# A fifth tile for the rows fetched by the first chunk's expert retrieval, in slots 16 to 59

## The chip, the core and the metric

The kernel runs on one core of one Trainium2 chip. The metric is the device time of one execution in microseconds (us); the median of 3 runs of the kernel before is 1491.55 us (1486.63 to 1492.42). Five engines work side by side, each through its own list of instructions in a fixed order: PE multiplies matrices into PSUM, DVE (VectorE) works element by element, ACT (ScalarE) evaluates functions, POOL (GpSimd) issues the indirect fetches and some small operations, and SP issues most of the plain transfers. Between the engines there are only semaphores; a transfer is split over 16 DMA engines that all queues share.

## The reference

One layer is computed for 512 prompt tokens and 32 sample tokens (8 sequences of 4), model width 1024, all in float32. The first half is a token mixer: one projection `w_in` gives q, k, v, a gate and two convolution inputs; four retention heads and a causal convolution of width 31 with a layer norm run beside each other; `w_out` brings both together, and a residual with layer norm gives x1. The second half is a product-key expert retrieval (PEER) on x1, followed by a residual and a layer norm:

```
q  = x1 @ w_query                           # 8 heads, 2 x 128 each
v1, i1 = top16(q1 @ sub_keys_1); v2, i2 = top16(q2 @ sub_keys_2)
sv, ci = top16(v1[:, None] + v2[None, :])   # 16 of 16 x 16 sums
idx  = i1[ci // 16] * 128 + i2[ci % 16]     # one of 16384 experts
act  = gelu(peer_u[idx] . x1)
ffn  = sum(softmax(sv) * act * peer_v[idx]) # over 8 x 16 = 128 slots a token
```

So each token uses 128 experts, one in each of 128 slots, and an expert is a row of `peer_u` and a row of `peer_v`, 4 KB each.

## The kernel before

**Two ways to do the retrieval.** The tokens are cut into four groups. For the first prompt chunk (128 tokens), the 32 sample tokens and the second prompt chunk (128 tokens) the kernel fetches rows: for slot k, one indirect DMA of POOL brings for each partition (a token) the row of u and v of its expert, 8 KB, into a tile `g` of 128 x 2048 (1 MB); DVE makes the dot product with x1 (L652), ACT the GELU (L663) and the gate (L664), and DVE adds the weighted v row to an accumulator `acc` (L669). That is 128 slots for the first chunk, 32 for the samples (four slots beside each other on 128 partitions) and 128 for the second chunk. For the last 256 prompt tokens the kernel computes all 16384 experts densely: scores against each block of 128 experts (`scores_of`, L913), weights scattered from the lists by one-hot products (`build`, L1040, with DVE making `A`, `M`, `B` and multiplying the result into the G tiles at L1069), and the product with v (`v_products`, L1097).

**Stages.** The front computes the mixer: the first chunk and the samples first, then the lists of the first chunk (`retrieve`, in pairs of heads), then the mixer of the remaining 416 columns. Its end is `mix_b`, four layer norms with transposes (L532) that give `x1T`. Then come the query projections and key scores for all later tokens, the top-16 lists, the dense scores of experts 52 to 95 (`early_keys`), then `first_keys` (experts 0 to 51, with the scattered weights for experts 0 to 95), and `phases`, the products with v and the last 32 blocks.

**The first chunk's slots.** `gather(x1_0, ...)` (L634) is a generator; the first KX = 48 slots are traced at the end of the front, the other 80 after the dense early part, ahead of `first_keys`. The order on each engine is made by a planner at build time that goes by order of tracing as priority and by its own estimate of durations, so that slots fill holes in the work of the front. A slot can be fetched as soon as its tile is free. The pool `gp` has three tiles, each fourth slot below KX takes the one tile of pool `gx`; from slot 48 on only `gp` is used. A fetch of slot k thus waits for the accumulation of slot k-4, later of k-3.

**hold.** `hold(k, ins)` (L630) puts all dot products of the first chunk from slot k on behind instruction `ins` on DVE: `conv_norm`'s last multiplication (slot 47), the head norms of chunks 2 and 3 (slots 48 and 52), and the four layer norms of `mix_b` (54, 56, 59, 60). It is an order on one engine without a semaphore.

**Memory.** Pools on the left side stand in the order `per`, `gp`, `gw`, then those of the front (`gx`, `fe`, `wk`), which are closed after the first KX slots are traced; on their place come `uvp` (the ring for blocks of u and v), the G tiles and the lists' scratch. On the right side lie `wp` (four weight tiles) and, before, `sel`: the scratch of the first chunk's lists and one tile `keys` of 8 KB for each partition, which later serves as room for states and for two of the layer norms. In `gather` the choice of tile is one line:

```
pool = gx if k < KX and k % 4 == 3 else gp
```

Of the kernel before, what the change touches and what calls it, by code (L numbers as in the profile page):

```python
# [8 lines left out]
F32 = mybir.dt.float32  # L9
# [11 lines left out]
D = 1024  # L21
# [11 lines left out]
ND = NR - NG2  # L33
TB = 8
GS = 2.0 ** 13
KX = 48
UV = 4
FREE = 30
TB_AT = (30, 34, 56, 80)
# [59 lines left out]
def tile_step(ctx: ExitStack, tc: tile.TileContext, a, o):  # L99
# [4 lines left out]
    gp = ctx.enter_context(tc.tile_pool(name="gp", bufs=3))  # L104
    gw = ctx.enter_context(tc.tile_pool(name="gw", bufs=3))
    wps, right = ExitStack(), ExitStack()
    wp = wps.enter_context(tc.tile_pool(name="wp", bufs=4, side="right", reuse_waits="tile"))
    sel = [right.enter_context(tc.tile_pool(name="sel", bufs=2, side="right"))]
    dr = ctx.enter_context(tc.tile_pool(name="dr", bufs=1, space=bass.MemoryType.DRAM))
    front = ExitStack()  # L110
    gx = front.enter_context(tc.tile_pool(name="gx", bufs=1, reuse_waits="tile"))
# [7 lines left out]
    def mmps():  # L119
        turn[0] += 1  # L120
        return banks[turn[0] % len(banks)].tile([128, 512], F32, name="mm")
# [50 lines left out]
    def behind(ins, other):  # L172
        tc.add_manual_dep(ins.ins, other.ins.name, mybir.DependencyInfo(
            mybir.DependencyClass.NoSync, mybir.DependencyReason.DATA), reason="order")
# [5 lines left out]
    def small(name, shape, dt=F32, bufs=2):  # L180
        return wk.tile(shape, dt, name=name, bufs=bufs)
# [117 lines left out]
    def conv_s(y, after):  # L299

        yp = y.rearrange("p m (b i) -> p m b i", b=SB)
        for k in range(CK):
            w = dw[:, :, k].unsqueeze(2).unsqueeze(3).to_broadcast([128, 4, SB, SQ])
            if k == 0:
                behind(G.tensor_tensor(yp, u_s[:, :, :, 0:SQ], w, op=OP.mult), after)
                G.tensor_tensor(y, y, dwb.unsqueeze(2).to_broadcast([128, 4, NS]), op=OP.add)
                continue
            t = small("tap_s", [128, 4, SB, SQ], bufs=1)
            G.tensor_tensor(t, u_s[:, :, :, k:k + SQ], w, op=OP.mult)
            G.tensor_add(yp, yp, t)  # L310

    def conv_norm(y, n):

        pm = mmps()
        for m in range(4):
            T.matmul(pm[:, :n], onesm, y[:, m, :n], start=(m == 0), stop=(m == 3))
        pv = mmps()
        for m in range(4):
            V.tensor_sub(y[:, m, :n], y[:, m, :n], pm[:, :n])
            sq = small("sg", [128, 416], bufs=1)  # L320
            S.activation(sq[:, :n], y[:, m, :n], AF.Square)
            T.matmul(pv[:, :n], onesm, sq[:, :n], start=(m == 0), stop=(m == 3))
        rs = small("ropeB", [128, 416], bufs=1)
        S.activation(rs[:, :n], pv[:, :n], AF.Sqrt, bias=eps_c)
        V.reciprocal(rs[:, :n], rs[:, :n])
        for m in range(4):
            last = V.tensor_mul(y[:, m, :n], y[:, m, :n], rs[:, :n])
            S.activation(y[:, m, :n], y[:, m, :n], AF.Silu, bias=cg_b[:, m:m + 1], scale=cg_g[:, m:m + 1])
        return last

    bv, steps = [None], {}
# [33 lines left out]
    def gate_heads(on, n, gT, c0):  # L365
        pt = mmps().rearrange("p (h t) -> p h t", h=H)
        for h in range(H):
            T.transpose(pt[:, h, :n], on[:n, h * DH:(h + 1) * DH], ident[:n, :n])
        V.tensor_mul(gT[:, :, c0:c0 + n], gT[:, :, c0:c0 + n], pt[:, :, :n])
# [164 lines left out]
        return last  # L534

    def keys_or_scratch():
        return sel[0].tile([128, 2 * D], F32, name="keys", bufs=1)

    keys = []

# [87 lines left out]
    def hold(k, ins):  # L628

        held[k] = ins  # L630

    def gather(x1, idx, gate, acc, slots):

        late = len(slots) == 128 and x1 is not x1_0  # L634
        for k in slots:
            if x1 is x1_0:
                pool = gx if k < KX and k % 4 == 3 else gp
            elif late:
                pool = (gp, gp, gp, gx2[0])[k % 4] if k < 60 else (gp, gp, gp, gx2[0], bx)[k % 5]
            else:  # L640
                pool = gp if k < FREE else (gp, gp, gp, gx2[0])[k % 4]
            t = pool.tile([128, 2 * D], F32, name="g")
            at = step(k) if late else -1
            while at >= len(marks):
                yield
            fetch = G.indirect_dma_start(out=t, out_offset=None, in_=a["uv"],  # L646
                                         in_offset=bass.IndirectOffsetOnAxis(ap=idx[:, k:k + 1], axis=0))
            if late:
                tc.add_manual_dep(fetch.ins, marks[at].ins.name, mybir.DependencyInfo(
                    mybir.DependencyClass.Sync, mybir.DependencyReason.DATA), reason="pace")  # L650
            act = gw.tile([128, 2], F32, name="act")
            dot = V.scalar_tensor_tensor(t[:, :D], t[:, :D], 1.0, x1, op0=OP.mult, op1=OP.mult, accum_out=act[:, 0:1])  # L652
            if x1 is x1_0:
                for k0, ins in held.items():
                    if k >= k0:
                        behind(dot, ins)
            elif fence and (late or k >= FREE):
                behind(dot, fence[0])
            if late and "rows" in steps:
                behind(dot, steps["rows"])  # L660
            dots.append(dot)
            wgt = gw.tile([128, 1], F32, name="wgt")
            S.activation(act[:, 1:2], act[:, 0:1], AF.Gelu)  # L663
            S.activation(wgt, act[:, 1:2], AF.Copy, scale=gate[:, k:k + 1])  # L664
            v = t[:, D:]
            if k == slots[0]:
                S.activation(acc, v, AF.Copy, scale=wgt)
            else:
                V.scalar_tensor_tensor(acc, v, wgt, acc, op0=OP.mult, op1=OP.add)  # L669
            yield  # L670
# [28 lines left out]
    for g, (w_, r_) in GSP.items():  # L699
# [9 lines left out]
    n = NR  # L709
    lead = gp.tile([128, 4, 4, 128], F32, name="g")  # L710
    y0, q0, k0, g0 = (lead[:, q] for q in range(4))
    qT, kT, gT, y = (blk[:, c0:c0 + 4 * w].rearrange("p (h t) -> p h t", h=4) for c0, w in (
        (0, n - NS), (4 * (n - NS), n - NS), (8 * (n - NS), n), (8 * (n - NS) + 4 * n, n)))
# [51 lines left out]
    for h0 in range(0, PH, 2):  # L765
        w = load_w(a["w_query"], h0 * 256)
        qq = small("qe", [128, 4, 128], bufs=1)
        for hs in ([h0], [h0 + 1]) if h0 == 0 else ([h0, h0 + 1],):
# [7 lines left out]
            c = V.tensor_copy(I0[:, ss], E0.rearrange("p h k -> p (h k)")[:, ss])  # L776
            led = led or [c]
    conv_s(yS, normed)

    def woven(large, small_):  # L780
        for _ in large:
            banks[:] = [ps0]
            next(small_, None)
            banks[:] = [ps]
        banks[:] = [ps0]
        for _ in small_:
            pass
# [24 lines left out]
    rope(load_win(1), 1, xT, n - NS, 160, [(0, n - NS, kT)])  # L812
    wg = load_win(3)
    S.activation(y[:, :, s_], yS, AF.Copy)
    hold(47, conv_norm(y, n))
    banks[:] = [ps0]
    ons = {}

    def before(c):
        c0 = C * (c - 1)  # L820
        return scores(qT, kT, c0), k_tokens(kT, c0, C, "p")

    def retain(c, sc, kt):
        c0 = C * (c - 1)
        po = attend(c, sc, qT, vs[c], c0)
        advance(c, kt, vs[c])
        ons[c] = head_norm(po, C, "p")

    retain(1, *before(1))
    retain(2, *before(2))  # L830
    hold(48, steps["p"])
    banks[:] = [ps]
    silu_gate(wg, xT, n - NS, [(0, n - NS, gT[:, :, r])], False)
    wo = load_w(a["w_out"], 0) + load_w(a["w_out"], 512)
    S.activation(gT[:, :, s_], gS, AF.Copy)
    banks[:] = [ps, ps, ps0, ps, ps0, ps, ps, ps0]
    xrs, pms, room = {}, {}, keys_or_scratch()

    def mix_a(c0, m, place):
        xrs[c0] = fe.tile([128, D], F32, name="xr0") if place is None else room[:, place * D:(place + 1) * D]  # L840
        if c0:
            pms[c0], _ = mix_mm(m, gT, y, c0, wo, x1T)
            return
        x1, pms[c0] = xrs[c0], None
        nc.scalar.dma_start(x1[:m], a["x"][128:128 + m])
        pm, _ = mix_mm(m, gT, y, c0, wo)
        for q in range(2):
            c = slice(q * 512, (q + 1) * 512)
            V.scalar_tensor_tensor(x1[:m, c], x1[:m, c], ALPHA, pm[q][:m], op0=OP.mult, op1=OP.add)

    def mix_b(c0, m):
        mix_norm(xrs[c0], m, x1T, c0, pms[c0])
        if c0 < NG2:
            nc.sync.dma_start(x1_dram[c0:min(c0 + m, NG2)], xrs[c0][:min(m, NG2 - c0)])
# [3 lines left out]
    caches()  # L858
    mix_a(0, NS, None)
    retain(3, *third)  # L860
    hold(52, steps["p"])
    gate_heads(ons[2], C, gT, NS + C)
    mix_a(NS, C, 0)
    gate_heads(ons[3], C, gT, NS + 2 * C)
    mix_b(0, NS)
    hold(54, steps["ln"])
    mix_a(NS + C, C, 1)
    mix_b(NS, C)
    hold(56, steps["ln"])
    mix_a(NS + 2 * C, C, None)  # L870
    mix_b(NS + C, C)
    hold(59, steps["ln"])
    mix_b(NS + 2 * C, C)
    hold(60, steps["ln"])
    gather0 = gather(x1_0, I0, g0_gates, acc0, range(PH * TK))
    for _ in range(KX):
        next(gather0)
# [69 lines left out]
    for g, (c0, m) in enumerate(DG):  # L947
# [9 lines left out]
        p = mmps().rearrange("p (q t) -> p q t", q=4)  # L957
# [187 lines left out]
    def step(k):  # L1145

        return k * 19 // 16
# [94 lines left out]
```

## Time and profile before

| | |
|---|---|
| median of 3 runs | 1491.55 us (1486.63 to 1492.42) |
| the profiled execution's own time | 1494.41 us |
| its span, first to last instruction | 1492.6 us |
| mean granted PE clock | 0.984 |
| busy: PE, DVE, ACT, POOL | 1427.4, 1169.0, 503.5, 425.6 us |
| moved by DMA | 503.63 MB, mean 337 GB/s |
| first chunk's fetches | 115.8 to 717.9 us |

The profile is one execution. In its tables a row names an instruction by engine, line and tiles (`out<-in`); "x" is a count. In the tables of stretches (from:to in us) each engine has its busy time and in brackets its instructions, then come the granted PE clock as a share, the share of time in which the DMA engines were busy, and GB/s. A table of waits says who waited for whom, with the sum in us, how often, and the longest. A timeline gives start, duration, engine and line, and in square brackets the idle time ahead of it with what ended it.

### The profile page before, as it was taken

How to read it: one execution, taken by the hardware profiler on the slowest of the kernel's cores; microseconds unless marked ns; L12 is line 12 of the kernel's file. 1: busy time of each engine (PE TensorE's matmuls, PEld its weight loads, DVE VectorE, ACT ScalarE, POOL GpSimd, SP SyncE). 2: the span in 40 equal slices, each digit the busy share in tenths (PEclk: the TensorE clock that was granted, in tenths of full speed). 3: DMA queues.
4: the chain of work that ended last, by engine and by line, in shares of the span. 5: the costliest groups of instructions: out<-in, count | busy, mean ns of one | idle time of the engine just before them, and what ended most of it. 6: DMA issues, size and time to landing. Idle time of an engine off the chain costs nothing.

```text
span 1492.6 us, 19525 instructions
## 1 busy us (share of the span) xinstructions
PE 1427.4 (96%) x6618; PEld 971.5 (65%) x6618; DVE 1169.0 (78%) x2875; ACT 503.5 (34%) x1495; POOL 425.6 (29%) x393
## 2 busy tenths in 40 slices
PE   8899999989899999998998999997999999999998
PEld 7878565557757578887877875443454666666443
DVE  5839958987748999998888997777989866666666
ACT  1424773362112222344544443113673111111110
POOL 2172214345322222222222220343333422222330
PEclk9999999999999999999999999998999999999999
DMA  9759769986899689999988984999999999999995
GB/s 347 296 189 370 245 224 355 390 292 235 316 378 357 245 304 347 349 362 345 316 339 332 334 300 167 361 423 400 339 374 389 408 418 408 412 404 407 413 411 194
DMA packets 99537, 503.63 MB, mean 337 GB/s; under 512 B 10183, under 2 KB 21191, under 8 KB 56549
## 3 DMA queue, kind: packets, MB, share of 16 engines
q0 software_dynamic: 42240, 305.12, 52.7%
q1 hardware_dynamic: 52157, 190.10, 33.5%
q10 hardware_dynamic: 5040, 7.16, 1.4%
q8 instruction: 52, 0.85, 0.2%
q14 instruction: 48, 0.39, 0.1%
HBM read 496.98 MB, written 5.80 MB: 337 GB/s over the span
## 4 chain that ended last, share of the span: by engine, by line
PE 49%; DVE 23%; DMA 17%; ACT 5%; issue 5%; POOL 1%; SPq 0%; DVEq 0%; ACTq 0%; POOLq 0%
PE pB L1097 18%; PE sp L913 12%; PE mm L216 11%; DMA g<-in_uv_dram,Ib 7%; DVE acc L669 6%; DVE g L652 5%; DMA g<-in_uv_dram,Is 4%; DMA g<-in_uv_dram,I 4%; PE mm L337 2%; ACT blk L282 2%; PE mm L521 2%; PE mm L1040 1%; PE mm L293 1%; POOL g L646 1%; DVE iu L551 1%
## 5 line engine op out<-in xcount | busy, mean ns | idle before, releaser
L913 PE MATMUL sp<-x1T,uv 128*128 128x256 f32 x2048 | 467.5, 384 | 2.8 <-ACT Gb L1055 1.5
L652 DVE SCALAR_TENSOR_TENSOR g<-g,x 128x1024 f32<-128x1024 f32 x288 | 350.7, 1218 | 105.5 <-DMA g<-in_uv_dram,I 48.6
L913 PEld LDWEIGHTS sp<-x1T,uv 128*128 128x128 f32 x2048 | 386.2, 192 | 69.4 <-issue 13.4
L669 DVE SCALAR_TENSOR_TENSOR acc<-g,wgt,acc 128x1024 f32<-128x1024 f32 x285 | 364.8, 1280 | 74.5 <-ACT wgt L664 73.2
L646 POOL DMA_INDIRECT g<-in_uv_dram,I x128 | 167.3, 1307 | 430.3 <-DVE acc L669 268.1
L646 POOL DMA_INDIRECT g<-in_uv_dram,Ib x128 | 161.4, 1261 | 358.6 <-PE pB L1097 123.8
L663 ACT ACTIVATE act<-act 128x1 f32<-128x1 f32 x288 | 57.9, 202 | 589.5 <-DVE g L652 589.1
L216 PE MATMUL mm<-x1T,w 128*128 128x384 f32 (+1 forms) x512 | 175.9, 501 | 0.0
L1097 PE MATMUL pB<-uv,Ga 128*128 128x512 f32 x352 | 158.2, 595 | 0.0
L216 PEld LDWEIGHTS mm<-x1T,w 128*128 128x128 f32 x512 | 96.8, 191 | 72.7 <-issue 40.8
L1097 PE MATMUL pB<-uv,Gb 128*128 128x512 f32 x256 | 111.8, 594 | 1.2 <-DMA uv<-in_uv_dram 0.8
L1097 PEld LDWEIGHTS pB<-uv,Ga 128*128 128x128 f32 x352 | 65.8, 190 | 69.2 <-issue 66.5
L1097 PE MATMUL pB<-uv,Gd 128*128 128x512 f32 x256 | 110.0, 592 | 0.0
L1097 PEld LDWEIGHTS pB<-uv,Gb 128*128 128x128 f32 x256 | 48.1, 190 | 62.3 <-issue 56.2
L1097 PEld LDWEIGHTS pB<-uv,Gd 128*128 128x128 f32 x256 | 48.6, 190 | 60.8 <-issue 59.3
L646 POOL DMA_INDIRECT g<-in_uv_dram,Is x32 | 39.2, 1224 | 147.3 <-DVE acc L669 31.4
L1016 ACT ACTIVATE off<-row,e1T 128x128 bf16<-128x128 bf16 x256 | 78.4, 392 | 1.8 <-PE mm L1040 1.4
L1097 PE MATMUL pB<-uv,Gc 128*128 128x512 f32 x160 | 75.4, 617 | 0.1
L1040 PEld LDWEIGHTS <-A 128*128 128x128 f16 x1024 | 45.0, 97 | 44.7 <-issue 25.1
L1053 ACT ACTIVATE W<-sp 128x256 f32<-128x256 f32 (+26 forms) x84 | 26.7, 318 | 126.5 <-PE sp L913 102.3
L1040 PE MATMUL mm<-B,A 128*128 128x96 f16 (+1 forms) x1024 | 48.9, 192 | 20.4 <-DVE Ga L1069 9.7
L216 PE MATMUL mm<-g,w 128*128 128x160 f32 (+1 forms) x512 | 65.4, 287 | 0.0
(293 smaller groups left out, 1594.3 us busy)
## 6 DMA issues: line engine op xcount, KB each, us to landing
uv<-in_ut_dram SPq DMA_DIRECT2D x128, 512.0 KB
uv<-in_uv_dram SPq DMA_DIRECT2D x128, 512.0 KB
w<-in_w_in_dram SPq DMA_DIRECT2D x18, 1024.0 KB
w<-in_w_query_dram SPq DMA_DIRECT2D x16, 1024.0 KB
w<-in_w_out_dram SPq DMA_DIRECT2D x7, 1024.0 KB
g<-in_uv_dram,I POOLq DMA_INDIRECT x128
g<-in_uv_dram,Ib POOLq DMA_INDIRECT x128
x1T<-in_xT_dram ACTq DMA_DIRECT2D x1, 1536.0 KB
```

The source lines that it names most:

```text
L216: T.matmul(p[:, :n], w[m // 2][:, k, (m % 2) * 128:(m % 2 + 1) * 128], xT[:, k, c0:c0 + n], start=(k == 0), stop=(k == 7))
L282: S.activation(rows[j * 32:j * 32 + 32, g], u_p[g * 32:g * 32 + 32, m, p0 + j:p0 + j + w], AF.Copy)
L337: mm = T.matmul(p[:n, q * 256:(q + 1) * 256], xT[:, k, c0:c0 + n], w[q][:, k, :], start=(k == 0), stop=(k == 7))
L521: last = T.matmul(banks_[q][:n, s * 256:(s + 1) * 256], src[:, k, c0:c0 + n], wo[q * 2 + s][:, k0 + k, :], start=(xT is None and k0 == 4 a ...
L646: fetch = G.indirect_dma_start(out=t, out_offset=None, in_=a["uv"], in_offset=bass.IndirectOffsetOnAxis(ap=idx[:, k:k + 1], axis=0))
L652: dot = V.scalar_tensor_tensor(t[:, :D], t[:, :D], 1.0, x1, op0=OP.mult, op1=OP.mult, accum_out=act[:, 0:1])
L663: S.activation(act[:, 1:2], act[:, 0:1], AF.Gelu)
L669: V.scalar_tensor_tensor(acc, v, wgt, acc, op0=OP.mult, op1=OP.add)
L913: mm = T.matmul(sp[:, i], u[:, k], x1T[:, k, NG2:], start=(k == 0), stop=(k == 7), skip_group_check=True)
L1016: S.activation(off[:, t], row, AF.Abs, bias=e1T[:, t1 + t:t1 + t + 1])
L1040: mm = T.matmul(pt[:, t % nt], A[t % TB], B[:, q, t % TB // 2, :, t % 2], start=(q == 0), stop=(q == 1))
L1097: return [T.matmul(pB[b][q], W[:, b * 128:(b + 1) * 128], vt[:, q * 512:(q + 1) * 512], start=False, stop=(e == NK - 1), skip_group_check= ...
```

## The change

A pool `kp` takes the tile `keys` out of `sel`. `sel` stands alone in a stack of its own, which is closed as soon as the convolution of the samples is traced, after the last list of the first chunk; in its place on the right side a pool `gx5` with one `g` tile opens. KX goes from 48 to 60. Slots 0 to 15 use four tiles as before; slots 16 to 59 go round five (three of `gp`, `gx`, `gx5`); from slot 60 on only `gp` is used. All slot numbers in `hold` go up by ten. No arithmetic and no transfer is added or taken away.

```
-KX = 48
+K5 = 16
+KX = 60
...
-    sel = [right.enter_context(tc.tile_pool(name="sel", bufs=2, side="right"))]
+    kp = [right.enter_context(tc.tile_pool(name="kp", bufs=1, side="right"))]
+    fifth = ExitStack()
+    sel = [fifth.enter_context(tc.tile_pool(name="sel", bufs=2, side="right"))]
...
     def keys_or_scratch():
-        return sel[0].tile([128, 2 * D], F32, name="keys", bufs=1)
+        return kp[0].tile([128, 2 * D], F32, name="keys", bufs=1)
...
             if x1 is x1_0:
-                pool = gx if k < KX and k % 4 == 3 else gp
+                pool = (gp, gp, gp, gx)[k % 4] if k < K5 else (gp, gp, gp, gx, gx5)[k % 5] if k < KX else gp
...
     conv_s(yS, normed)
+    fifth.close()
+    gx5 = right.enter_context(tc.tile_pool(name="gx5", bufs=1, side="right", reuse_waits="tile"))
...
-    hold(47, conv_norm(y, n))
+    hold(57, conv_norm(y, n))
...
-    hold(48, steps["p"])
+    hold(58, steps["p"])
...
-    hold(52, steps["p"])
+    hold(62, steps["p"])
...
-    hold(54, steps["ln"])
+    hold(64, steps["ln"])
...
-    hold(56, steps["ln"])
+    hold(66, steps["ln"])
...
-    hold(59, steps["ln"])
+    hold(69, steps["ln"])
...
-    hold(60, steps["ln"])
+    hold(70, steps["ln"])
```

## The prediction

> **What bounds the kernel now.** I read the page's busy times first, then the stretches between the kernel's stages.
>
> ```profile
> span 1492.6 us, 19525 instructions
> ...
> PE 1427.4 (96%) x6618; PEld 971.5 (65%) x6618; DVE 1169.0 (78%) x2875; ACT 503.5 (34%) x1495; POOL 425.6 (29%) x393
> ...
> 204.00:346.00 142.00, 135.51 (x687) 83.62 (x680) 124.45 (x213) 66.85 (x163) 52.60 (x42) 0.98 0.89 338
> 346.00:409.00 63.00, 56.93 (x307) 49.09 (x306) 49.45 (x78) 9.83 (x35) 29.59 (x23) 0.96 0.72 268
> 409.00:466.00 57.00, 57.00 (x196) 34.08 (x195) 30.14 (x38) 12.51 (x40) 15.50 (x12) 0.98 0.98 377
> 466.00:660.00 194.00, 192.18 (x853) 153.29 (x852) 188.58 (x686) 60.39 (x165) 48.00 (x40) 1.00 0.87 323
> 660.00:740.00 80.00, 75.32 (x464) 65.59 (x463) 67.85 (x136) 34.29 (x140) 21.07 (x18) 0.98 0.91 334
> 740.00:912.00 172.00, 160.34 (x989) 133.75 (x987) 142.89 (x326) 75.78 (x303) 37.41 (x31) 0.98 0.82 303
> ...
> 1045.00:1365.00 320.00, 319.60 (x1389) 189.03 (x1388) 245.04 (x472) 101.01 (x312) 93.30 (x78) 1.00 1.00 396
> ```
>
> PE works 1427.4 of 1492.6 us, and none of its work is touched. So the change can only act through the 65 us in which PE stands, and through PE's clock. From 1045 on PE does not stand (319.60 of 320): whatever is won or lost before 912 goes through to the end as it is. DVE is full from 466 to 660 (188.58 of 194), while PE, on dense scores, waits for nothing there. Next, who PE waits for, from 204 on.
>
> ```profile
> PE mm L532 <- DVE xr L503: 6.1, 1, 6.1
> PE mm L521 <- ACT ktok L377: 4.7, 1, 4.7
> ...
> PE pB L508 <- ACT Ga L943: 2.0, 1, 2.0
> PE mm L1040 <- ACT e2T L967: 1.8, 1, 1.8
> ...
> PE mm L1040 <- DVE Ga L1069: 8.9, 5, 2.9
> PE sp L913 <- ACT Gb L1055: 1.5, 1, 1.5
> ...
> PE mm L1040 <- DVE B L1024: 8.8, 2, 6.3
> ```
>
> The first two lie in the front, the next two from 660 to 740, the 8.9 and 1.5 from 740 to 912 (`first_keys`), and the 8.8 near 1035. Most of them are waits for DVE, which carries the slots. That is the whole field on which the change can play.
>
> **How many slots the fifth tile brings forward.** Dots are counted by stretch (two instructions each, the dot and the reading of its sum), with what DVE waited for fetches in three of these stretches, the cost of an accumulation, and POOL's wait for free tiles from 204 to 410.
>
> ```profile
> 115.00:204.00 89.00, 15.98 (x27) 0.97 0.74 278
> 204.00:346.00 142.00, 42.60 (x70) 0.98 0.89 338
> 346.00:409.00 63.00, 15.47 (x25) 0.96 0.72 268
> 409.00:466.00 57.00, 15.22 (x26) 0.98 0.98 377
> ...
> DVE g L652 <- DMA g<-in_uv_dram,I: 7.0, 8, 2.2
> ...
> DVE g L652 <- DMA g<-in_uv_dram,I: 11.3, 5, 4.4
> ...
> DVE g L652 <- DMA g<-in_uv_dram,I: 21.1, 7, 5.9
> ...
> L669 DVE SCALAR_TENSOR_TENSOR acc<-g,wgt,acc 128x1024 f32<-128x1024 f32 x285 | 364.8, 1280 | 74.5 <-ACT wgt L664 73.2
> ...
> POOL g L646 <- DVE acc L669: 119.0, 37, 20.1
> ```
>
> A slot costs DVE 42.60/35 = 1.22 us plus 1.28, so 2.5 us. By 409 there are (27+70+25)/2 = 61 dots, slots 0 to 60. Nearly every fetch waits for an accumulation to free its tile (119.0 us, 37 times), so the tiles do set the pace of the fetches. But DVE only loses what it waits for a fetch: 7.0 us with four tiles (at most 7.0/2.5 = 3 slots) and 11.3 us with three (4 to 5 slots). Those are the least to be reckoned with; all of DVE's idle time in both stretches, 17.55 + 13.55 = 31.1 us, would be 12 slots, the most. The transfers stand against the first stretch (DMA busy 0.89) and not against the second (0.72). I take 2 + 3 = **5 slots, 12.5 us of DVE work** that is done before 409 and not after it; bounds 0 and 12. From 409 to 466 three tiles and full DMA engines (0.98) stay as they are.
>
> **The change part by part.** Moving `keys` to `kp` issues nothing new. The fifth tile waits for the list scratch in its place, and the first of `uvp` for whatever of `gx` it covers:
>
> ```profile
> 218.31 1.68 POOL L646 DMA_INDIRECT g<-in_uv_dram,I  x1 [0.92 <-DVE acc L669]
> ...
> 401.39 8.67 SPq L911 DMA_DIRECT2D uv<-in_ut_dram  x4
> ```
>
> Slot 19 is the first in `gx5` and is fetched at 218.31, past the stretch up to 204 in which I take the lists to be made (I have no row for the scratch's last use): 0 us, or, were it freed late, one fetch's wait. `gx` is now in use up to slot 58, not 47. If `uvp` lies on it, SP's load at 401.39 waits for that slot's accumulation, at 396.13 in the timeline below: 0 us, with 5 us to spare. Behind it on SP stand the query weights, for which PE would wait. POOL issues the same 288 fetches; its small norm operations stand behind fetches that wait less, 0.
>
> What is left are the four places where PE waits for DVE. First the end of the front, in DVE's timeline, with the granted clock behind the wait, and the last wait of `first_keys` with its clock:
>
> ```profile
> 396.13 1.27 DVE L669 SCALAR_TENSOR_TENSOR acc<-g,wgt,acc 128x1024 f32<-128x1024 f32 x1
> ...
> 400.99 1.23 DVE L652 SCALAR_TENSOR_TENSOR g<-g,x 128x1024 f32<-128x1024 f32 x1 [2.26 <-DMA g<-in_uv_dram,I]
> ...
> 402.82 1.28 DVE L669 SCALAR_TENSOR_TENSOR acc<-g,wgt,acc 128x1024 f32<-128x1024 f32 x1 [0.60 <-ACT wgt L664]
> 404.02 1.29 DVE L489 BATCH_NORM_STATS2 lst<-mm 128x6 f32<-128x512 f32 x2
> ...
> 406.92 1.40 DVE L503 SCALAR_TENSOR_TENSOR xr<-xr,lrs,lnb 128x512 f32<-128x512 f32 x2
> 408.24 1.22 DVE L652 SCALAR_TENSOR_TENSOR g<-g,x 128x1024 f32<-128x1024 f32 x1
> ...
> 413.44 1.22 DVE L652 SCALAR_TENSOR_TENSOR g<-g,x 128x1024 f32<-128x1024 f32 x1 [3.97 <-DMA g<-in_uv_dram,I]
> ...
> 419.66 1.23 DVE L652 SCALAR_TENSOR_TENSOR g<-g,x 128x1024 f32<-128x1024 f32 x1 [4.99 <-DMA g<-in_uv_dram,I]
> ...
> 420.81 4.07 DVE L669 SCALAR_TENSOR_TENSOR acc<-g,wgt,acc 128x1024 f32<-128x1024 f32 x3
> ...
> 404.00:411.00 7.00, 3.20 (x11) 2.41 (x12) 5.39 (x10) 1.58 (x4) 1.75 (x3) 0.51 1.00 418
> 888.70:892.10 3.40, 3.40 (x8) 2.71 (x9) 3.40 (x9) 1.71 (x6) 0.00 (x0) 0.50 0.33 136
> ...
> 887.83 0.51 PE L1040 MATMUL mm<-B,A 128*128 128x96 f16 x8 [2.02 <-DVE Ga L1069]
> ```
>
> - **End of the front, L532.** The dot at 400.99 is slot 59's. It waits 2.26 us for its rows, its accumulation 0.60 more, and the last layer norm stands behind both. With an earlier fetch these go: -2.9, and about -1.0 of the time at half clock (0.51 over 7 us; at most 3.4 us are lost there). Bounds: -9.5 (6.1 + 3.4), and a loss, which is a rival below.
> - **660 to 740.** DVE being full until 660, what stands behind the first chunk's slots comes up to 12.5 us earlier. The wait for e2T (1.8), whose inputs DVE makes, goes; the 2.0 for Ga is dense scores and ACT, and stays. -1.8, bounds 0 and -3.8.
> - **740 to 912.** The samples' slots follow the first chunk's and start up to 12.5 us earlier, so some leave this stretch at its end: the last wait (2.02) and its window at half clock (3.4/2 = 1.7) go, the four others stay, as they come from single slots between single L1069: -3.7, of which I take -3, since the planner mixes the operations anew. Bounds +4 (two more waits like this) and -14 (8.9 + 1.5, two windows of clock).
> - **Near 1035.** The second chunk's slots are issued after `first_keys`, so this wait moves along: 0. Were it to change by itself, -9 to +6.
>
> The trace has PE at half clock after a wait of only 2.02 us. The Trainium skill (TensorE: Matmul & The Clock Gate, "What's actually happening") has PE fall to half rate after an idle window of about 3.4 us; by that rule the 2.02 us wait would cost nothing beyond itself, and the third term would be 1.7 us smaller. I go by the row.
>
> **Sum.** -2.9 - 1.0 - 1.8 - 3 = **-8.7 us**. The profiled execution took 1494.41 us, 2.9 over the median: from it 1485.7, from the median of 1491.55 us 1482.9. I say **1484**, with 1477 to 1491 for this case.
>
> **The rivals.**
>
> *The fetches were not the limit.* DMA is busy 0.89 of the time while four tiles turn, and a fifth place makes no bandwidth. Then perhaps two slots come forward, every wait stays, 1491.55 - 2 = **1490**. For it: DVE waited just 7.0 us there. Against it: the second stretch, where DMA is idle 0.28 of the time and the number of tiles goes from three to five. The Trainium skill (DMA: Bandwidth & Descriptors, "Issuing engines are not separate DMA queues") says that transfers of all issuers interleave on the same 16 engines, so that more fetches could also delay weights; no PE wait on weights stands among those above.
>
> *Slower: slots 60 to 62 get ahead of the last layer norm.* `hold` kept them behind it; with 70 in its place slots up to 69 are free, and these three are fetched with three tiles amid the query weights. The dots at 408.24, 413.44 and 419.66 with their accumulations, done by 424.88, are 12.6 us from 408.24 to 420.81 in which DVE mostly waits. Ahead of the norm they would keep PE from `x1T`: +12.6, one more window at half clock +1.7, less the later terms (-4.8): 1491.55 + 9.5 = **1501**. It decides from two such dots on (413.44 + 1.22 - 408.24 = 6.4 us, more than the 4.8 won later). Against it: the planner puts the norm first where it believes both ready; for it: it cannot know how late these rows come.
>
> *More is won.* All waits for DVE from 400 to 912 go, 6.1 + 1.8 + 8.9 = 16.8, with clock windows (3.4 and one of 1.7) 21.9: **1470**. It needs nearly all 12 slots.
>
> *ACT pays.* With `hold` at 57 instead of 47, GELUs may fall between the sigmoids and the norm of the convolution. A change of function table costs 1.283 us:
>
> ```profile
> L264 ACT ACT_TABLE_LOAD x4 | 5.1, 1283 | 0.1
> ```
>
> PE already waits 4.7 us for ACT there. Each further GELU between two other functions is 2.57 us; four would be 10.3 and eat the gain: 1491.55 + 10.3 - 8.7 = **1493**.
>
> **How the numbers follow.** About 0.5% (7.5 us) is what a measurement of this kernel tells from no change: faster means below 1484.1, slower above 1499.0. Forecast 0.41, of which 0.25 is faster and 0.16 within; more won 0.15, faster; fetches not the limit 0.19, with 0.02 faster, else within; ACT 0.08, with 0.01 slower; slots ahead of the norm 0.17, slower. Together faster 0.42, within 0.40, slower 0.18. The range goes to the cases on both sides, 1469 to 1502, with about a tenth left out on either side.
>
> **What would show it.** Dots until the transposes of the last norm: 61 before, 66 by the forecast. The wait of L532 for L503: 6.1 before, about 3; over 12 would be the slower rival. The last fetch of the first chunk stands some 12 us earlier. L1040's waits for L1069 from 740 to 912: 8.9 before, 7 or less. The wait for `ktok` and the table loads until 346 should not grow. If the first four hold and the time does not move, the wait near 1035 has taken it back. The forecast is wrong if the number of dots by 409 does not rise, or if the planner's new mixing moves waits by more than the 9 us in the sum.

## The result and the profile after

The changed kernel takes 1500.97 us in the median of 10 runs (1495.41 to 1504.59); the kernel before, beside it, 1491.99 us (1483.43 to 1496.48). The ratio is **1.0064, with a 95% interval of 1.0042 to 1.0086**: slower, by about 9 us. Forecast was 1484; the time of the rival "slots 60 to 62 get ahead of the last layer norm" was 1501.

In the changed kernel all lines lie lower: the dot is L655 (before L652), the accumulation L672 (L669), the fetch L649 (L646), the layer norm's last step L506 (L503) and its transposes L535 (L532), the one-hot products L1045 (L1040), their factor `B` L1029 (L1024). The profiled execution took 1503.6 us. The page's span and busy times after:

```profile
span 1501.5 us, 19538 instructions
...
PE 1428.2 (95%) x6618; PEld 970.3 (65%) x6618; DVE 1166.6 (78%) x2875; ACT 502.4 (33%) x1496; POOL 427.9 (28%) x393
```

PE and DVE work as long as before (1427.4 and 1169.0). Of the 8.9 us of span, 8.1 are standing time of PE. Whom PE waits for, after:

```profile
PE mm L535 <- DVE xr L506: 18.5, 2, 16.9
PE mm L1045 <- DVE B L1029: 9.6, 2, 7.0
PE mm L1045 <- DVE Ga L1074: 7.1, 9, 2.2
...
PE mm L524 <- ACT ktok L380: 3.9, 1, 3.9
...
PE mm L1045 <- ACT e2T L972: 0.8, 1, 0.8
```

The first row is the loss: one wait of 16.9 us for the last layer norm, where there was one of 6.1. None of the other rows shown is more than 1 us above before, and most are smaller. The same in stretches; the columns are those of the table before:

```profile
404.00:425.00 21.00, 4.10 (x20) 3.22 (x19) 12.76 (x18) 3.91 (x12) 4.00 (x5) 0.58 1.01 422
409.00:466.00 57.00, 43.87 (x138) 25.81 (x139) 26.26 (x35) 10.49 (x33) 12.59 (x11) 0.83 0.82 317
...
740.00:912.00 172.00, 165.67 (x1039) 140.89 (x1039) 141.91 (x327) 76.67 (x314) 36.84 (x29) 0.99 0.81 301
...
1045.00:1365.00 320.00, 316.38 (x1380) 185.66 (x1380) 243.36 (x484) 104.19 (x321) 94.40 (x76) 0.99 0.98 389
```

From 404 to 425 PE works 4.10 us of 21, and its granted clock is 0.58. From 409 to 466 it lost 13.1 us against before (57.00 of 57). From 740 to 912 it has 165.67 us where it had 160.34, so it wins 5.3 there, and from 1045 to 1365 it loses 3.2 (316.38, before 319.60). What DVE does in the gap, in its timeline (start, duration, what ended the idle time ahead of it):

```profile
399.84 1.41 DVE L506 SCALAR_TENSOR_TENSOR keys<-keys,lrs,lnb 128x512 f32<-128x512 f32 x2
407.63 1.22 DVE L655 SCALAR_TENSOR_TENSOR g<-g,x 128x1024 f32<-128x1024 f32 x1 [6.38 <-DMA g<-in_uv_dram,I]
...
408.79 0.69 DVE L492 BATCH_NORM_STATS2 lst<-mm 128x6 f32<-128x512 f32 x1
...
412.60 1.23 DVE L655 SCALAR_TENSOR_TENSOR g<-g,x 128x1024 f32<-128x1024 f32 x1 [1.85 <-DMA g<-in_uv_dram,I]
...
417.58 1.23 DVE L655 SCALAR_TENSOR_TENSOR g<-g,x 128x1024 f32<-128x1024 f32 x1 [1.01 <-DMA g<-in_uv_dram,I]
...
418.73 1.41 DVE L501 SCALAR_TENSOR_TENSOR xr<-mm,lmv,lng 128x512 f32<-128x512 f32 x2
...
421.24 1.41 DVE L506 SCALAR_TENSOR_TENSOR xr<-xr,lrs,lnb 128x512 f32<-128x512 f32 x2
```

These are the dots of slots 63, 64 and 65. Their rows come at 407.6, 412.6 and 417.6, and the parts of the last layer norm (L492, L501, L506) stand between them and behind them. In the order on DVE each of these parts waits for a fetch that it has nothing to do with. POOL's issues of these fetches:

```profile
396.29 1.94 POOL L649 DMA_INDIRECT g<-in_uv_dram,I  x1 [9.30 <-DVE lmv L493]
...
399.35 1.50 POOL L649 DMA_INDIRECT g<-in_uv_dram,I  x1 [0.18 <-issue]
401.16 0.96 POOL L649 DMA_INDIRECT g<-in_uv_dram,I  x1 [0.30 <-issue]
```

The first of them waits for a free tile: three tiles go round there, so slot 63 takes that of slot 60, whose accumulation DVE makes from 394.75 to 396.02 us, 7.4 us after the end of slot 60's dot (the profile names `lmv`, which ends at nearly the same time). The rows take 11.3, 13.3 and 16.4 us from the start of the issue. The chain of work that ended last goes over the third of them, and then over the norm to PE:

```profile
401.16 16.39 DMA g<-in_uv_dram,I
...
417.58 0.04 DVE g L655
...
422.13 1.94 PE mm L535 x8
```

Four points of the timelines show what becomes of the delay, in us from the start of the span (e13 and e14 are experiments, below):

| | before | after | e13 | e14 |
|---|---|---|---|---|
| last transpose of the last layer norm | 409.3 | 423.7 | 423.5 | 408.4 |
| first one-hot product (L1040, L1045) | 672.7 | 687.1 | 686.3 | 675.6 |
| 41st product with v | 922.0 | 926.8 | 931.3 | 920.2 |
| end of the last product with v | 1485.4 | 1494.3 | 1495.8 | 1487.1 |

After stands 14.4 us behind at the first point and at the second, 4.8 at the third, 8.9 at the end.

### The profile page after: what moved, and what is told of

The parts are those of the page before. It is cut to its first block, busy times and chain, and to the rows that moved or that the text cites. A ratio compares the mean times of both kernels' runs of the same rounds, so it can differ in the third digit from the quotient of the medians.

```text
span 1501.5 us, 19538 instructions
## 1 busy us (share of the span) xinstructions
PE 1428.2 (95%) x6618; PEld 970.3 (65%) x6618; DVE 1166.6 (78%) x2875; ACT 502.4 (33%) x1496; POOL 427.9 (28%) x393
## 4 chain that ended last, share of the span: by engine, by line
PE 44%; DVE 23%; DMA 18%; ACT 6%; issue 5%; POOL 3%; ACTq 0%; DVEq 0%; SPq 0%; POOLq 0%
PE pB L1102 21%; PE sp L918 12%; PE mm L219 8%; DMA g<-in_uv_dram,I 7%; DVE acc L672 7%; DMA g<-in_uv_dram,Ib 5%; DVE g L655 5%; DMA g<-in_uv_dram,Is 4%; ACT blk L285 2%; POOL g L649 1%; DMA uv<-in_ut_dram 1%; PE mm L1045 1%; PE mm L524 1%; DVE iu L554 1%; DVE B L1029 1%
## 5 line engine op out<-in xcount | busy, mean ns | idle before, releaser
L672 DVE SCALAR_TENSOR_TENSOR acc<-g,wgt,acc 128x1024 f32<-128x1024 f32 x285 | 364.7, 1280 | 90.7 <-ACT wgt L667 90.2
L655 DVE SCALAR_TENSOR_TENSOR g<-g,x 128x1024 f32<-128x1024 f32 x288 | 350.6, 1219 | 92.8 <-DMA g<-in_uv_dram,Ib 45.4
L649 POOL DMA_INDIRECT g<-in_uv_dram,I x128 | 165.3, 1291 | 428.2 <-DVE acc L672 234.8
L649 POOL DMA_INDIRECT g<-in_uv_dram,Ib x128 | 164.6, 1286 | 359.0 <-PE pB L1102 127.9
L649 POOL DMA_INDIRECT g<-in_uv_dram,Is x32 | 41.0, 1281 | 157.4 <-DVE M L1025 43.4
L1045 PEld LDWEIGHTS <-A 128*128 128x128 f16 x1024 | 43.5, 97 | 41.0 <-issue 22.5
L219 PEld LDWEIGHTS mm<-g,w 128*128 128x128 f32 x512 | 64.4, 191 | 0.7
L1045 PE MATMUL mm<-B,A 128*128 128x96 f16 (+1 forms) x1024 | 47.4, 191 | 17.6 <-DVE B L1029 9.6
```

The source lines that it names most:

```text
L219: T.matmul(p[:, :n], w[m // 2][:, k, (m % 2) * 128:(m % 2 + 1) * 128], xT[:, k, c0:c0 + n], start=(k == 0), stop=(k == 7))
L1045: mm = T.matmul(pt[:, t % nt], A[t % TB], B[:, q, t % TB // 2, :, t % 2], start=(q == 0), stop=(q == 1))
```

## The experiments

All ratios are to the kernel before, run beside each, with 95% intervals. Unless a base is named, an edit is made on the changed kernel.

### Are the shifted holds the loss, or the fifth tile?

**e3: the holds alone**, on the kernel before, without the fifth tile. The changed lines of `hold` are written as one, here and below.

```
-    hold(47 / 48 / 52 / 54 / 56 / 59 / 60, ...)
+    hold(57 / 58 / 62 / 64 / 66 / 69 / 70, ...)
```

> The kernel before, four tiles up to slot 47 and three after it, with only the holds' slot numbers raised by ten. On DVE 62 dots then stand ahead of the last norm's statistics instead of 60, and 63 ahead of its last step. Theory A: PE's wait for the last norm grows from 6.1 to 12 to 19 us, as the rows of slots 60 to 62 come late at three tiles, and the time goes to 1498 to 1505 us; the fifth tile is then not what costs. Theory B: the shift alone costs less than 3 us, below 1495 us.

Measured 1.010 (1.007 to 1.013). PE's wait:

```profile
PE mm L532 <- DVE xr L503: 15.5, 1, 15.5
```

The whole loss is there without the fifth tile, and with nearly the same wait (15.5 us, after 16.9).

**e13: the last hold alone**, on the kernel before: one number.

```
-    hold(60, steps["ln"])
+    hold(70, steps["ln"])
```

> The kernel before with one number changed: the last hold from 60 to 70, so that nothing keeps slots 60 and later behind the last layer norm; no fifth tile, the other six holds as they were. Theory (slots fetched with three tiles get ahead of the last layer norm, and this alone is the loss): the wait of L532 for L503 grows from 6.1 to 12 us or more, as with all holds shifted (15.5), and the ratio to before is near 1.007 to 1.010. Rival (it takes the shift of the earlier three layer norms too): a wait of under 8 us, or a longer wait with a ratio of 0.998 to 1.003.

Measured 1.0083 (1.0052 to 1.0115). Waits of PE, first row, and then the stretch around it:

```profile
PE mm L532 <- DVE xr L503: 18.7, 1, 18.7
```

```profile
404.00:425.00 21.00, 3.02 (x10) 2.40 (x11) 12.64 (x17) 3.86 (x11) 4.67 (x6) 0.55 1.02 423
```

One number of seven carries it: the long wait and the stretch at half clock come with this hold alone.

**e14: the last hold back at 60**, the other six shifted, the fifth tile in place.

```
-    hold(70, steps["ln"])
+    hold(60, steps["ln"])
```

> The changed kernel with one number changed: the last hold from 70 to 60, the other six shifted by ten and the fifth tile as in the change. Theory: all of the loss goes, the wait of L535 for L506 is about 2.4 us, ratio to before 0.998 to 1.002, no better than with all four layer norms at their old slots (0.9995). Rival (the earlier three norms cost as well): ratio 1.004 or more, with the mix's last product later than 406 us.

Measured 1.001 (0.9989 to 1.0032). Waits of PE:

```profile
PE mm L566 <- ACT score L568: 5.5, 1, 5.5
...
PE mm L535 <- DVE xr L506: 3.7, 2, 2.4
```

The loss is gone, so the other six holds cost nothing that can be told. And although the last norm is now waited for 2.4 us instead of 6.1 at the longest, the kernel is no faster than before; in its profile a wait of 5.5 us for `score`, at 567 us, is new.

**e1: the last hold at 63.** With it slots 60 to 62, which five tiles have brought in time, stay ahead of the last norm.

```
-    hold(70, steps["ln"])
+    hold(63, steps["ln"])
```

> The changed kernel with one number altered: the last layer norm of the front is held ahead of slot 63 on (70 in the change), so that on DVE the dots of slots 63 to 65 stand behind it, all else in the front as changed. Theory A (the three dots, whose rows come late, keep the last layer norm and with it PE back): PE's wait for the last norm falls from 16.9 us to 6 or less, the half clock behind it to one window or none, and the time from 1501 to 1486 to 1490 us, which is below the kernel before. Theory B (the fifth tile slows the front in other ways, since PE has finished the mixer's products at 405 instead of 401.7 us): the wait falls but at least half of the 9 us loss stays, 1495 us or more.

Measured 1.0018 (0.9999 to 1.0038). Waits of PE:

```profile
PE mm L1045 <- ACT e2T L972: 6.1, 1, 6.1
PE mm L325 <- ACT sg L324: 5.6, 3, 4.7
PE mm L535 <- DVE xr L506: 4.3, 2, 2.4
```

The loss goes here too, but for what may be a small rest. Theory A wanted the kernel faster than the one before, and it is not. Two waits for ACT that were 1.8 and 2.7 before are 6.1 and 5.6 now.

**e2: all holds at their old numbers.**

```
-    hold(57 / 58 / 62 / 64 / 66 / 69 / 70, ...)
+    hold(47 / 48 / 52 / 54 / 56 / 59 / 60, ...)
```

> The changed kernel with all seven slot numbers of the holds as they were before (47, 48, 52, 54, 56, 59, 60); the fifth tile stays. 60 dots stand ahead of the last norm, as before. Theory A: PE's wait for the last norm is 3 to 6 us, and the time lies between 1486 and 1493 us, no more than 1 us better than the kernel before if the fifth tile cannot be used without the later holds. Theory B: slower than before by 3 us or more although the holds are the old ones.

Measured 0.9988 (0.9967 to 1.0008): the fifth tile alone brings nothing that this measurement can tell from no change. Waits of PE:

```profile
PE mm L1045 <- ACT act L666: 10.4, 1, 10.4
...
PE mm L535 <- DVE xr L506: 2.4, 1, 2.4
```

**e11: only the four layer-norm holds at their old numbers**, the first three shifted.

```
-    hold(64 / 66 / 69 / 70, steps["ln"])
+    hold(54 / 56 / 59 / 60, steps["ln"])
```

> The changed kernel with the three holds ahead of the layer norms as in the change (57, 58, 62) and the four on the layer norms as before (54, 56, 59, 60). If the holds on the layer norms are what costs, this is as fast as the one with all old holds: 1484 to 1492 us, wait for the last norm 2 to 6 us. If the first three cost by GELUs between the sigmoids, 3 to 6 us more.

Measured 0.9995 (0.9976 to 1.0015), with 2.4 us of waiting for the last norm. **e12: as e2, but the last hold at 63.**

```
-    hold(60, steps["ln"])    # of e2
+    hold(63, steps["ln"])
```

> The changed kernel with all holds as before but the last one, which is at 63 instead of 60: slots 60 to 62, fetched with five tiles' distance by 392 us, go ahead of the last norm's statistics. They are there in time, so the wait for the last norm stays at 2 to 4 us and the time at 1483 to 1492 us. Three more dots done early are worth 1 us at most by the run with five slots fewer.

Measured 1.0022 (0.9998 to 1.0047), the same wait of 2.4 us, and 5.1 us for e2T.

### Why do the rows come late?

**e4: the first four loads of u behind the last layer norm**, so that they don't run beside the fetches of slots 63 to 65.

```
+    last_norm = steps["ln"]
...
-            nc.sync.dma_start(u, a["ut"][e + i])
+            load = nc.sync.dma_start(u, a["ut"][e + i])
+            if e < E0S[2] + 4 and e >= E0S[2]:
+                await_(load, last_norm)
```

> The changed kernel, with the first four loads of u blocks (512 KB each) waiting for the last layer norm instead of running beside the fetches of slots 63 to 65; DVE's order is unaltered. If those fetches are late because they share the transfer engines with 4 MB of query weights, 2 MB of u, keys and norm rows (all busy from 396 to 424 us), a fifth to a quarter of the traffic goes: PE's wait for the last norm falls from 16.9 to about 12 to 14 us, the time to 1496 to 1499 us, as long as u still lands before PE wants it some 15 us later. If the rows are late for another reason (the issue on POOL, a tile that is not free), the wait stays within 1 us of 16.9.

Measured 1.008 (1.0048 to 1.0112). The three dots in DVE's timeline:

```profile
414.85 1.22 DVE L655 SCALAR_TENSOR_TENSOR g<-g,x 128x1024 f32<-128x1024 f32 x1 [6.95 <-DMA g<-in_uv_dram,I]
...
419.82 1.23 DVE L655 SCALAR_TENSOR_TENSOR g<-g,x 128x1024 f32<-128x1024 f32 x1 [1.86 <-DMA g<-in_uv_dram,I]
...
424.80 1.22 DVE L655 SCALAR_TENSOR_TENSOR g<-g,x 128x1024 f32<-128x1024 f32 x1 [1.02 <-DMA g<-in_uv_dram,I]
```

They still come 5 us apart, and PE's wait is 16.6 us. The u loads are not the cause, and could hardly be: in the changed kernel they stand behind the query weights in SP's queue. Among the packets of that queue the first of u starts at 415.7 us, when two of the three rows have come and the third is due at 417.6. So this run took away a load that was not yet there, and says nothing on what sharing costs. What is left beside the fetches are the query weights (4 MB, issued by SP at 403.28 there, at 395.75 in the changed kernel); without them PE has no work behind the norm, so they were not taken away. That they make the rows late is not shown by a run of its own, and neither is what the late accumulation of slot 60 costs.

**e5: five tiles up to slot 65**, with the dots of slots 62 to 65 ahead of the last norm.

```
-KX = 60
+KX = 66
...
-    hold(69, steps["ln"])
+    hold(66, steps["ln"])
...
-    hold(70, steps["ln"])
+    hold(66, steps["ln"])
```

> The changed kernel with five tiles up to slot 65 instead of 59, and the last three holds at 66, so that 66 dots stand ahead of the last norm's statistics (in the change 63 to 65, its last ones between the steps). Theory A (rows of slots 63 to 65 are late because at three tiles they can be fetched only when slots 60 to 62 are done, just as the query weights start to load): they are now fetched some 8 to 15 us earlier, ahead of those loads, PE's wait for the last norm falls from 16.9 to 8 us or less, and the time to 1486 to 1494 us. Theory B (so many dots ahead of the norm cost by their own 2.5 us each, whatever the fetches do): the wait stays at 12 us or more and the time at 1497 or more.

Measured 1.0105 (1.0063 to 1.0146). Waits of PE:

```profile
PE mm L535 <- DVE xr L506: 9.4, 2, 7.9
```

The wait falls from 16.9 to 7.9 us, but most of that is PE coming later to it: it begins to wait at 412.7 us (405.2 after) and goes on at 420.7 (422.1 after). The three fetches start at 396.33, 398.68 and 402.72 us, not earlier than after (396.29, 399.35, 401.16), though earlier beside the query weights, which are issued from 402.04 on (395.75 after). With that the rows are there in time: from 405 to 421 us no dot waits for a fetch. What is left of the wait is DVE's own work, dots and accumulations one behind the other, with the norm's last statistics behind them at 417.48 us. So each theory has a part of it, and the time does not fall. PE's last product of the mixer, which the norm stands behind, is at 410.3 us in this profile (404.0 after, 400.5 before). That alone can't be the loss, as it is at 411.1 in e1, whose time is that of the kernel before. Over all the profiles here that point lies between 398.4 and 411.9 us, and what moves it was not tried by itself; so where e5 loses stays open.

### What is a lead of DVE worth?

**e6: five slots fewer**, on the kernel before: slots 96 to 100 are left out of the first chunk. So the samples' slots follow 12.5 us sooner, as the forecast wanted it of the fifth tile. The lists of the second chunk, whose place is counted in dots, fall five slots later by it.

```
-    gather0 = gather(x1_0, I0, g0_gates, acc0, range(PH * TK))
+    gather0 = gather(x1_0, I0, g0_gates, acc0, [k for k in range(PH * TK) if not 96 <= k <= 100])
```

> The kernel before without slots 96 to 100 of the first chunk: five fetches, dots and accumulations are left out, 12.5 us of DVE work and 5 MB, so that the output is not the reference's; everything up to the end of the front stays. It measures what 12.5 us less DVE work after the front is worth. The forecast had two terms for it, 1.8 us from 660 to 740 and 3 us from 740 to 912: if these were right, the time falls by 4 to 6 us to 1482 to 1485. If DVE's lead is worth nothing because PE's waits there come from single operations, by less than 2 us. If it is worth more than I sized, as the changed kernel's shorter way from the scattered weights to the products with v suggests (10 us), by 8 to 11 us.

Measured 0.9991 (0.9973 to 1.0009). Waits of PE:

```profile
PE mm L1040 <- ACT act L663: 9.7, 1, 9.7
```

That wait ends at 1039 us; before, a wait of 6.3 us for `B` ended at 1037.5. The product reads `A` and `B` and not `act`, and in DVE's timeline `B` is made just ahead of it, behind the dot of a slot that waited for its rows:

```profile
1037.51 1.23 DVE L652 SCALAR_TENSOR_TENSOR g<-g,x 128x1024 f32<-128x1024 f32 x1 [0.58 <-DMA g<-in_uv_dram,Ib]
...
1038.66 0.49 DVE L1024 TENSOR_TENSOR B<-M,gtT 128x256 f16<-128x256 f16 x2
```

So it is a wait for `B` here too, though the profile names `act`. The lead is worth less than 2 us by the ratio, and no more than 4 by its interval.

**e9: twenty slots fewer** (90 to 109 left out), 50 us of DVE work; the lists of the second chunk keep their place.

```
-    gather0 = gather(x1_0, I0, g0_gates, acc0, range(PH * TK))
+    gather0 = gather(x1_0, I0, g0_gates, acc0, [k for k in range(PH * TK) if not 90 <= k <= 109])
...
-            if len(dots) - 128 in TB_AT:
-                lists_b(TB_AT.index(len(dots) - 128))
+            if len(dots) - 108 in TB_AT:
+                lists_b(TB_AT.index(len(dots) - 108))
```

> The kernel before without slots 90 to 109 of the first chunk (20 fetches, dots and accumulations left out: 50 us of DVE work and 20 MB, the output is not the reference's), the points at which the second chunk's lists are made kept in step. The ceiling of what a lead of DVE after the front can give. Theory P (PE's own work from the front's end to the products with v, some 503 us, sets the time and DVE's waits are its jitter): no more than 10 us faster, 1481 us or more, with the scattered weights to products stretch near 239 us (249 before). Theory D (DVE's load bounds that stretch): 15 us faster or more.

Measured 1.0000 (0.9975 to 1.0024). A stretch, and the first wait of PE:

```profile
740.00:912.00 172.00, 170.99 (x1025) 138.36 (x1024) 122.67 (x357) 76.97 (x289) 14.42 (x12) 1.00 0.60 211
```

```profile
PE mm L1040 <- ACT act L663: 11.2, 1, 11.2
```

With 50 us less for DVE, PE does win where the forecast looked for it: 170.99 us of work from 740 to 912 instead of 160.34. It then stands 11.2 us until 1026.8 (again ahead of a product of `A` and `B`), where before it stood 8.8 in two waits around 1035, and the median does not move. This one profile was 10 us under its own median (1479.69 against 1489.74), so its waits are not to be taken for the typical run's.

### Does a delay go through, and do single numbers move the rest?

**e10: PE later by work of its own**, on the kernel before: four query projections are made once more, their results unused.

```
+        for m in range(4 if h0 == 0 else 0):
+            project(w, m, x1T, 0, n)
```

> The kernel before with 32 further matmuls of 416 columns ahead of the query projections, their result unused: PE comes 11.2 us later to all that follows the front, DVE does not. It measures how much of a delay at the front's end is taken up later. In the changed kernel the first scattered weights were 14.4 us later and the products with v 4.8 us. If a delay is taken up by the waits for DVE from there on, the time grows by 2 to 5 us; if not, by 9 to 12.

Measured 1.0201 (1.0169 to 1.0232). The expectation's 11.2 us was too small: a float32 product is two instructions in the trace, and the group of projections grew from 256 instructions and 91.1 us to this:

```profile
L216 PE MATMUL mm<-x1T,w 128*128 128x416 f32 x320 | 113.9, 517 | 0.9 <-ACT score L565 0.9
```

That is 22.8 us more, and the medians stand 26.9 apart. Against its true size the delay is whole in the time, with nothing of it absorbed. On the way it is not constant: in this profile the first one-hot product, at 710.9 us, is 38.2 later than before, and the 41st product with v, at 948.5, is 26.5 later.

**e7: numbers between the old and the new.**

```
-    hold(57 / 58 / 62 / 64 / 66 / 69 / 70, ...)
+    hold(47 / 48 / 52 / 56 / 58 / 61 / 63, ...)
```

> The changed kernel with holds between the old and the new ones (47, 48, 52, 56, 58, 61, 63): the first three as before, then 63 dots ahead of the last norm. By theory A the wait for the last norm is 2 to 5 us; slots 60 to 62 are fetched by 392 us and done before it. Time 1483 to 1490 us, at best 0.3% under the kernel before. If instead the mixer's end moves (PE's last mixer product after 405 us), 1488 to 1493 us.

Measured 1.0088 (1.0058 to 1.0117). Waits of PE:

```profile
PE mm L1045 <- DVE B L1029: 11.2, 2, 7.8
...
PE mm L535 <- DVE xr L506: 5.8, 2, 3.4
PE mm L964 <- DVE e L961: 4.7, 2, 4.1
```

**e8: the same idea, with five tiles up to slot 65.**

```
-KX = 60
+KX = 66
...
-    hold(57 / 58 / 62 / 64 / 66 / 69 / 70, ...)
+    hold(47 / 48 / 53 / 56 / 58 / 62 / 64, ...)
```

> As the one before with five tiles up to slot 65 and holds 47, 48, 53, 56, 58, 62, 64. A candidate for a better version: 64 dots ahead of the last norm with their rows there in time, wait for the last norm 2 to 5 us, and two more slots done early. 1481 to 1488 us if the lead of DVE is worth 1 to 2 us for each slot; no different from the kernel before if it is not.

Measured 1.0042 (1.0019 to 1.0066), with 2.6 us of waiting for the last norm (2.4 in e7, where the 3.4 in the row above belongs to an earlier norm). Both have no long wait at the last norm, and both are slower than before. In e7 the loss is spread over waits that had other sizes before (`e` 4.1, `B` 7.8). That the planner orders the rest anew with each number is argued from these rows; no run held that order fixed. What e7 loses by stays open.

No kernel here beats the one before: the best, e2 and e11, are the same as it within the measurement.

## Why the prediction was wrong, by its steps

**What bounds the kernel: right.** PE's work did not change, and 8.1 of the 8.9 us are PE's standing time. In e10 a delay of PE behind the front is whole in the time; that what is won or lost before 912 us goes through to the end as it is holds only within some us: in the changed kernel PE is 4.8 us behind at the 41st product with v and 8.9 at the end.

**Five slots forward: the size was off.** By 409 the dots, with the readings of their sums, after:

```profile
115.00:204.00 89.00, 16.62 (x27) 0.98 0.78 290
204.00:346.00 142.00, 43.01 (x72) 0.96 0.89 338
346.00:409.00 63.00, 18.28 (x30) 0.99 0.80 287
409.00:466.00 57.00, 11.07 (x18) 0.83 0.82 317
```

(27 + 72 + 30)/2 is 64, not 66; 3 slots instead of 5, inside the bounds. The last fetch of the first chunk starts at 711.9 us, 6.0 earlier and not 12, since in the gap from 409 to 466 DVE gets through 9 slots where it did 13.

**The end of the front (-2.9 and -1.0): the step that failed.** It measured +14.4, of which the wait is 10.8 (16.9 - 6.1) and 3.5 that the mixer's last product comes later (404.0 against 400.5; in e6, e9 and e10, whose edits do not touch the front, that point lies between 398.4 and 406.3); with the last hold back at 60 the wait shrinks as the step wanted (2.4, e14), but the step costed a hold that was no longer there. Its error is the choice between two cases. The prediction wrote down this very mechanism as a rival, with price and condition, and gave it 0.17 because "the planner puts the norm first where it believes both ready". The trace shows three slots put ahead of it; a fetch that is late gives its dot no later place in a fixed order. The row for it was already before the prediction: the dots at 413.44 and 419.66, which waited 3.97 and 4.99 us. What kept them harmless was the hold at 60, and the change took it away. A fence that is moved has to be priced as taken away for the slots between its old place and its new one.

**The slower rival: right in mechanism and time, off in its parts.** It had slots 60 to 62; with the three slots gained it was 63 to 65, and the mechanism is the same: three fetches with three tiles amid the query weights. Its +12.6 measured 10.8. Its half-clock window (+1.7) is there too. Stretches around the end of the wait, after, and then the one of before in which the transposes begin:

```profile
408.00:422.00 14.00, 0.00 (x0) 0.00 (x0) 10.51 (x16) 2.46 (x8) 3.08 (x5) 0.50 1.01 422
422.00:425.40 3.40, 3.27 (x10) 2.41 (x11) 2.12 (x4) 1.58 (x4) 0.92 (x1) 0.50 1.00 411
425.40:428.80 3.40, 3.40 (x8) 1.74 (x7) 1.58 (x2) 0.00 (x0) 0.95 (x1) 0.63 1.04 423
428.80:435.00 6.20, 6.20 (x19) 3.41 (x18) 2.57 (x4) 0.50 (x2) 0.94 (x1) 1.00 1.02 418
```

```profile
407.80:411.20 3.40, 3.40 (x11) 2.57 (x12) 1.66 (x3) 1.58 (x4) 0.00 (x0) 0.55 1.01 419
```

By the granted clock, 3.4 x 0.50 + 3.4 x 0.37 = 3.0 us of work are lost after the wait, before 3.4 x 0.45 = 1.5: 1.5 more. The later terms, -4.8, measured -9.6 up to the 41st product with v (14.4 behind at the first point of the table, 4.8 at the third); 4.1 are lost again by the end. The sum, +9.5, measured 8.9 between the profiles. That they come so near is in part luck: 3.5 us in the front and 4.1 at the end, which the rival did not have, make up for later gains twice as large as it priced.

**660 to 740 (-1.8) and 740 to 912 (-3): the rows moved, the time did not follow.** After, e2T is waited for 0.8 us (before 1.8), and PE works 5.3 us more from 740 to 912. But a lead of DVE brings no time that can be told: e6 and e9 give it 12.5 and 50 us and measure 0.9991 and 1.0000. In e9 the gain in that stretch is there, 10.7 us more work of PE, and the wait near 1030 is longer. The step priced the waits of one stretch and took it that nothing behind it gives the gain back. The window at half clock that it saw behind a wait of 2.02 us shows again after: a wait of 2.22 us ends at 854.0 us, and the clock is 0.53 from 854.8 to 858.2.

**Near 1035 (0): held in the changed kernel, not in e2, e6 and e9.** After, PE waits 9.6 us there for `B` (8.8 before). In e2, e6 and e9 it is in the main one wait, of 10.4, 9.7 and 11.2 us, ending at 1040.3, 1039.0 and 1026.8 us. What it stands behind can be read from the traces: DVE makes `B` behind the first dots of the second chunk, 24 of them before and in e6, 25 in e2, 26 in e9. Towards the end most of these come 3.7 us apart and wait for their rows, and the DMA engines are full (1.02 from 960 to 1000 us, before and in e9). In e9 the first of these dots comes 20.6 us earlier than before (926.45 against 947.06), but with two more of them ahead the wait ends just 10.7 us earlier. That is the pattern of the front's end once more: work for PE in fixed order behind dots whose rows are still to come. No run changed this order, so what it costs is not shown.

**The moves that cost nothing: right.** PE waits for no load between 400 and 912 us, so `uvp` in the place of `gx` held up nothing that it needs, and POOL's busy time is 427.9 us against 425.6. **"The fetches were not the limit"** at 1490 is close to what the fifth tile alone gives (e2, 0.9988), but not by its reason: the tile does bring the fetches forward, slot 59's dot from 401.0 to 381.8 us, and it is the lead that is worth nothing. **"ACT pays": refuted**, as `ktok` is waited for 3.9 us, 0.8 less than before. ACT loads one function table more until 346 us (30, before 29), but so it does in e2 and e11, which are as fast as the kernel before.

## What to carry to other kernels

Before moving a fence on an in-order engine, list what the fence held back and look up in the trace when the data of those operations arrive: an operation whose transfer is late holds everything behind it, and its price is that arrival minus the moment at which the held-back work was ready. Shift only the fences whose position the change has earned; here one number of seven made the loss, and a run that changes it alone shows it. And try what a lead of a helper engine is worth by leaving some of its work out before building a way to win it: 50 us of it were worth nothing here that could be told (1.0000, 0.9975 to 1.0024).

## What the runs showed of the hardware

**Beside the query weights the fetches get about half of the moving data.** Three fetches of 1 MB issued within 5 us land 5.0 us apart (407.6, 412.6, 417.6), so at some 210 of 422 GB/s, and again 5.0 apart in e4, beside the same 4 MB of query weights. Transfers by queue from 396 to 420 us, after (packets, MB, share of 16 engines):

```profile
q1 hardware_dynamic: 696, 4.68, 53.8%
q0 software_dynamic: 550, 4.09, 41.2%
```

The Trainium skill (DMA: Bandwidth & Descriptors, "Queues, rings and completion order") has each DMA engine take turns between the queues that have work, packet by packet; the trace agrees, 4.09 MB for the fetches beside 4.68 for SP's loads. The share is not one half everywhere: in the kernel before, from 960 to 1000 us, the fetches moved 10.64 MB in 1468 packets and SP's queue 6.24 MB in 1715 smaller ones, and the dots come 3.7 us apart there. What a smaller load of the other queue does to a fetch was not measured; in e5, where the first two of the three fetches are issued ahead of the query weights, no dot from 405 to 421 us waits for its rows.

**The clock after a long wait.** It is 0.50 from 408 us to the end of the wait at 422, 0.50 and 0.63 in the next two stretches of 3.4 us, then full. The Trainium skill (TensorE: Matmul & The Clock Gate, "What's actually happening") gives the gate a free-running window of about 3.4 us, a busy one of which releases the clock; the rows agree, full speed having come between 425.4 and 428.8, 3.3 to 6.7 us after PE began at 422.1.
